# A split-precision transformer layer on one core: three of four right-hand sums of the way down on VectorE, in place, with other slots for the tiles around them

## The chip, the core and the metric

The kernel runs on one core of a Trainium2 chip. The metric is the device time in microseconds (us) of one execution, as the median of several. The engines are TensorE (PE, matrix products), VectorE (DVE), ScalarE (ACT), GpSimd (POOL), and SyncE (SP), which here issues all transfers. Each works through a queue of its own strictly in order and waits for the others by semaphores. Operands lie in an on-chip buffer of 128 partitions; the results of matrix products lie in eight accumulation banks of 128x512 numbers.

## The reference

The program is one layer of a transformer on 1024 tokens of width 1024: two kinds of attention, a gated merge, a normalization, and a feed-forward network (FFN) with a hidden width of 2816. Only the FFN's second half, the "way down", is touched:

```python
g, u = jnp.split(x @ w_ffn_in[l], 2, axis=-1)
ffn = (jax.nn.silu(g) * u) @ w_ffn_out[l]
x = layer_norm(DEEPNORM_ALPHA * x + ffn, ln2_g[l], ln2_b[l])
```

Everything is float32.

## The kernel before

**Split precision.** A float32 product is emulated by three fast ones. Each operand is split into a high part (a cast on ScalarE, line 108) and a low part (the operand minus its high part, on VectorE, line 109), and high x high, high x low and low x high are summed in a bank. The weights of the plain products are split the same way in a helper (line 402 is its subtraction).

**The way up.** The hidden activations h come in 22 tiles f of 128 units (0 to 21). Each is made by seven half-size products instead of eight (the Strassen-Winograd scheme), at line 170 into the banks named sxf, syf and szf. VectorE adds them up at line 183 into the tiles gt and h; lines 830, 833 and 834 are the last steps of silu(g) * u. The left sums of h for the way down are made and written out to a DRAM buffer s_dr in the course of this stage.

**The way down** (lines 906 to 1027) comes in three stages. First plain: f = 0 and 1, eight tiles of tokens x two halves x 6 matmuls, into banks of the tags mm and tr; VectorE evacuates each bank with alpha * x + bank (line 1009). Then four groups of sevens, for f = 2 to 5, 6 to 9, 10 to 13 and 14 to 17. Each group has two pairs of f (named by their first: 2 and 4, 6 and 8, 10 and 12, 14 and 16) and two halves of the tokens; each half runs seven products in the order 1, 2, 6, 5, 7, 3, 4 of 12 matmuls (line 995, banks dx, dy, dz), and VectorE adds each bank to x (line 925). Then plain again: f = 18 to 21, with a normalization for each tile of tokens.

**The right sums.** A seven needs, for each pair of f, the raw weights L (the lower columns of rows f and f+1 of w_ffn_out, side by side) and R (the upper columns), and four sums of them, each split into a high and a low part. The generator right_sums makes them. Before the change it loads L and R into tiles of the tag gt, and POOL makes the four sums (lines 950, 951, 953, 954) in two further tiles, tda and tdb, of the tag yt. The split parts are wdl (raw L), wdb and wda (the sums) and wdc (the upper half of R, raw). The generator stops at each yield; it is moved on by two steps after each tile of the first plain stage and by one step after each product of the sevens, one group ahead.

**The order and the slots.** The order on each engine follows the order of the program text, with a scheduler that moves instructions by their dependencies. All tiles of 128x1024 numbers come from pools by tag, each with so many slots (bw 9, pt 4, yt 3, gt 3, kp 4, xt 16, and qs, kh, kl, v with 2 each, together called QKV). A tile that takes a slot waits until the last reader of the slot's previous tile is done. So the tag of a tile decides what it waits for. The tag gt also holds gt21 of the last f, xt and QKV hold operands of the way up (the products 5 and 7 read theirs, x1S57, from QKV).

Of the kernel before, what the change touches and what calls it, by code (L numbers as in the profile page):

```python
# [26 lines left out]
NF = D_FF // P  # L27
# [4 lines left out]
LO, HI = slice(0, HW), slice(HW, 2 * HW)  # L32
# [14 lines left out]
def hybrid_trunk_kernel(ctx: ExitStack, tc, x, xt, w_in, b_gate, rel_bias, w_proj,  # L47
# [6 lines left out]
    nc = tc.nc  # L54
# [7 lines left out]
    def slot(tag, name, dtype=F32):  # L62
        return pool.tile([P, 1024], dtype, tag=tag, name=name, bufs=SLOTS[tag])
# [8 lines left out]
    QKV = ("qs", "kh", "kl", "v")  # L72
# [34 lines left out]
    def split(dst_h, dst_l, src):  # L107
        nc.scalar.copy(dst_h, src)  # L108
        nc.vector.tensor_tensor(dst_l, src, dst_h.bitcast(F32), ALU.subtract)  # L109
# [571 lines left out]
    for si, (hd, g, st, box) in enumerate(vsteps):  # L681
# [12 lines left out]
        last = goal  # L694
# [182 lines left out]
    for half_k in range(2):  # L877
# [6 lines left out]
        for tt in range(8):  # L884
# [8 lines left out]
            if half_k == 1:  # L893
# [9 lines left out]
              first=3, aside=next_piece)  # L903
# [4 lines left out]
    def load_plain(f0, f1, tags):  # L908
        hs = []
        take = lambda name, dtype: cycle(tags, name, dtype)  # L910
        for f in range(f0, f1):
            hs.append(load_w(h_dr[f], f"h{f}", of("gt"), take, nc.vector) +
                      load_w(w_ffn_out[f * P:(f + 1) * P, :], f"fo{f}", of("gt"), take,
                             nc.vector))
        return hs
# [11 lines left out]
    def right_sums(g, Ws, tags):  # L927

        def take(name):
            return cycle(tags, name, F32R)  # L930

        def split_to(W, key, src, nm):
            W[key] = take(f"{nm}h"), take(f"{nm}l")
            split(*W[key], src)

        def load(W, f, key, cs):
            t = W[key] = slot("gt", f"wd{key}{f}")
            for j, dst in enumerate((LO, HI)):
                dma(t[:, dst], w_ffn_out[(f + j) * P:(f + j + 1) * P, cs])

        sub = ALU.subtract
        put = nc.gpsimd.tensor_tensor
        for f, W in zip(SEVEN[g], Ws):
            load(W, f, "L", LO)
            split_to(W, "hl", W["L"], f"wdl{f}")
            yield
            load(W, f, "R", HI)
            L, R = W["L"], W["R"]
            ta, tb = slot("yt", f"tda{f}"), slot("yt", f"tdb{f}")
            put(ta[:, LO], R[:, LO], L[:, LO], sub)  # L950
            put(tb[:, LO], R[:, HI], ta[:, LO], sub)
            yield
            put(tb[:, HI], L[:, HI], tb[:, LO], sub)
            put(ta[:, HI], R[:, HI], R[:, LO], sub)
            yield
            split_to(W, "hb", tb, f"wdb{f}")
            yield
            split_to(W, "ha", ta, f"wda{f}")
            yield
            c = W["c"] = take(f"wdc{f}")  # L960
            split(c[:, LO], c[:, HI], R[:, HI])
            yield

    def load_left(g, hf):
# [6 lines left out]
    def down_seven(g, hf, Ws, ls, between):  # L971

        bx, by = {}, {}
        key = {1: ("hl", LO), 2: ("hl", HI), 5: ("ha", LO), 7: ("ha", HI), 6: ("hb", LO),
               4: ("hb", HI)}
        for p in ORDER:
            for j in range(2):
                tt = 2 * hf + j
                nm = f"{g}_{tt}"
                up, lo = acc_t[tt], acc_t[tt + 4]  # L980
                if p == 1:
                    bx[j] = bank(("mm", "tr")[hf], f"dx{nm}")
                elif p in (2, 5):
                    by[j] = bank("sc" if p == 5 else ("tr", "pv")[j], f"d{'yz'[p == 5]}{nm}")
                acc = by[j] if p in (2, 5, 3) else bx[j]
                first = p in (1, 2, 5)
                for i, W in enumerate(Ws):
                    if p == 3:
                        wh, wl = W["c"][:, LO], W["c"][:, HI]
                    else:  # L990
                        wh, wl = (w[:, key[p][1]] for w in W[key[p][0]])
                    o = i * HW + j * P
                    lh, ll = ls[p][:, o:o + P], ls[p][:, o + 256:o + 256 + P]
                    for n, (a, b) in enumerate(((lh, wh), (lh, wl), (ll, wh))):
                        mm(acc, a, b, start=(first and i == n == 0), stop=(i == n - 1 == 1),  # L995
                           skip_group_check=not first)
                for dst in {1: [up[:, LO]], 2: [up[:, LO]], 6: [up[:, HI]], 5: [lo[:, HI]],
                            7: [lo[:, HI]], 3: [up[:, HI]], 4: [lo[:, LO]]}[p]:
                    add_to(dst, acc)
            between()  # L1000

    LEFT = ("bw",) * 5 + ("kp",) * 2 + ("bw",) * 4 + ("kp",) * 2
    right_tags = [("xt",) * 14, QKV * 2 + ("pt",) * 4 + ("xt",) * 2]
    first = load_plain(0, 2, ("bw",) * 2 + ("kp",) * 2)
    Wd = [[dict(), dict()] for _ in SEVEN]
    make = right_sums(0, Wd[0], right_tags[0])
    for tt in range(8):
# [6 lines left out]
    for g in range(4):  # L1014
        if g < 3:
            make = right_sums(g + 1, Wd[g + 1], right_tags[(g + 1) % 2])
        for hf in range(2):
# [1 line left out]
            if (g, hf) != (3, 1):  # L1019
                left = load_left(g + hf, 1 - hf)  # L1020
            down_seven(g, hf, Wd[g], ls, lambda: next(make, None))
    last = load_plain(18, NF, ("xt",) * 14 + ("bw",) * 2)
    norm2 = [bcast(src, slot("yt", f"ln2{n}")) for src, n in ((ln2_g, "g"), (ln2_b, "b"))]
    for tt in range(8):
        down_plain(last, tt, add_to)
# [36 lines left out]
```

## Time and profile before

| | before |
|---|---|
| median of 3 runs | 1499.21 us (1498.03 to 1502.22) |
| the profiled execution's own time | 1501.38 us |
| its span in the profile | 1499.3 us |
| mean granted TensorE clock | 0.993 |
| TensorE busy | 1440.3 us, 96% |
| VectorE busy | 1043.9 us, 70% |
| ScalarE busy | 679.7 us, 45% |
| POOL busy | 282.4 us, 19% |

The profile is one execution. Its page gives busy times, the span in 40 slices, and the chain of work that ended last. Beside it stand views of the trace: waits (an engine, the line and tile that waited, what it waited for, us in total, times, longest), the timeline of an engine (start, duration, engine, line, operation, output<-inputs, sizes; in brackets the idle time ahead of it and what ended it), and windows (the busy time of each engine in a stretch, with the granted clock). Buffer numbers are left out of names there: wl_fo is wl_fo0 or wl_fo1. Durations of consecutive instructions of one engine overlap a little; their pitch is read from starts.

### The profile page before, as it was taken

How to read it: one execution, taken by the hardware profiler on the slowest of the kernel's cores; microseconds unless marked ns; L12 is line 12 of the kernel's file. 1: busy time of each engine (PE TensorE's matmuls, PEld its weight loads, DVE VectorE, ACT ScalarE, POOL GpSimd, SP SyncE). 2: the span in 40 equal slices, each digit the busy share in tenths (PEclk: the TensorE clock that was granted, in tenths of full speed). 3: DMA queues.
4: the chain of work that ended last, by engine and by line, in shares of the span. 5: the costliest groups of instructions: out<-in, count | busy, mean ns of one | idle time of the engine just before them, and what ended most of it. 6: DMA issues, size and time to landing. Idle time of an engine off the chain costs nothing. (4 is left out here: it accounts for less than half of the span.)

```text
span 1499.3 us, 19075 instructions
## 1 busy us (share of the span) xinstructions
PE 1440.3 (96%) x6728; PEld 1179.6 (79%) x6728; DVE 1043.9 (70%) x1702; ACT 679.7 (45%) x1174; POOL 282.4 (19%) x322
## 2 busy tenths in 40 slices
PE   8999999999999999899999899999999998999997
PEld 6788888887887777777787688888888886778886
DVE  8865556435878887887849966767777755767757
ACT  6444444336877778775303534444444433111201
POOL 0000000004344558650014000000000003341016
PEclk9999999999999999999999999999999999999999
DMA  6555555247754556647502123444444456677602
GB/s 211 163 175 169 168 168 170 98 144 213 206 170 142 159 165 204 187 157 280 183 0 87 62 100 121 152 155 155 155 155 154 155 189 232 245 249 267 234 8 105
DMA packets 81215, 244.05 MB, mean 163 GB/s; under 512 B 10064, under 2 KB 10064, under 8 KB 81120
## 3 DMA queue, kind: packets, MB, share of 16 engines
q1 hardware_dynamic: 81120, 242.84, 48.5%
q8 instruction: 53, 0.87, 0.2%
q14 instruction: 42, 0.34, 0.1%
HBM read 162.03 MB, written 80.77 MB: 162 GB/s over the span
## 5 line engine op out<-in xcount | busy, mean ns | idle before, releaser
L535 POOL TENSOR_TENSOR w_b<-w_b,kp_b 128x511 f32<-128x511 f32 (+3 forms) x96 | 97.5, 1021 | 51.5 <-DVE kp_b L533 40.6
L950 POOL TENSOR_TENSOR tda<-wdR,wdL 128x512 f32<-128x512 f32 x8 | 10.7, 1340 | 491.6 <-DMA wdR<-in_w_ffn_out_dram 477.8
L533 DVE TENSOR_TENSOR_SCAN kp_b<-kp_b,ident_ps 128x384 f32<-128x384 f32 (+6 forms) x88 | 78.3, 890 | 4.1
L479 POOL MEMSET bias<- 64x64 f32 x8 | 1.2, 146 | 334.5 <-ACT bias L478 334.5
L745 POOL TENSOR_TENSOR mv<-mv,neghalf 128x1 f32<-128x1 f32 x16 | 23.9, 1495 | 211.4 <-DVE mv L744 211.4
L525 ACT ACTIVATE kp_b<-sc_b 128x512 f32<-128x512 f32 (+3 forms) x96 | 48.5, 505 | 31.4 <-PE sc_b L462 26.5
L183 DVE TENSOR_TENSOR c<-sxp,c 128x512 f32<-128x512 f32 x16 | 11.1, 692 | 73.9 <-issue 40.7
L925 DVE TENSOR_TENSOR x<-dx,x 128x512 f32<-128x512 f32 x64 | 43.6, 689 | 24.6 <-PE dx L995 24.6
L109 DVE TENSOR_TENSOR pt_b<-tp_b,pt_b 128x512 fp32r<-128x512 f32 (+1 forms) x96 | 51.1, 543 | 10.9 <-ACT pt_b L108 10.4
L170 PE MATMUL szf<-x1S63h,wcf 128*128 128x512 f32 x176 | 57.8, 389 | 0.0
L500 POOL TENSOR_SCALAR w_a<-w_a,st_a 128x640 f32<-128x640 f32 (+2 forms) x64 | 42.6, 671 | 67.2 <-DVE st_a L499 49.6
L556 PE MATMUL tp_b<-ident,w_b 128*128 128x128 f32 x288 | 49.3, 277 | 5.2 <-DVE pt_b L109 2.8
L108 ACT CAST pt_b<-tp_b 128x512 fp32r<-128x512 f32 (+1 forms) x96 | 47.1, 497 | 13.7 <-PE tp_b L556 13.2
L109 DVE TENSOR_TENSOR sl<-h,sl 128x512 fp32r<-128x512 f32 x56 | 38.4, 686 | 20.2 <-ACT sl L108 20.2
L108 ACT CAST sl<-h 128x512 fp32r<-128x512 f32 x56 | 34.8, 621 | 35.6 <-PE syf L170 17.1
L109 DVE TENSOR_TENSOR pt_a<-tp_a,pt_a 128x512 fp32r<-128x512 f32 (+1 forms) x96 | 45.5, 484 | 7.6 <-ACT pt_a L108 7.3
L497 ACT ACTIVATE w_a<-w_a,st_a 128x640 f32<-128x640 f32 (+2 forms) x64 | 44.6, 698 | 12.8 <-DVE st_a L492 11.2
L118 PE MATMUL ops<-wh_o,ml 128*128 128x512 f32 x128 | 50.2, 392 | 0.2 <-DVE ml L109 0.2
L115 PE MATMUL ops<-wh_o,mh 128*128 128x512 f32 x128 | 50.2, 392 | 0.0
L116 PE MATMUL ops<-wl_o,mh 128*128 128x512 f32 x128 | 49.9, 390 | 0.0
L556 PE MATMUL tp_a<-ident,w_a 128*128 128x128 f32 x240 | 44.8, 277 | 5.0 <-POOL w_a L500 2.4
L833 ACT ACTIVATE h<-sxf 128x512 f32<-128x512 f32 x22 | 13.2, 598 | 79.6 <-PE sxf L170 79.6
(1881 smaller groups left out, 4833.4 us busy)
## 6 DMA issues: line engine op xcount, KB each, us to landing
s_dr<-sl SPq DMA_DIRECT2D x112, 256.0 KB, 2.2
sd<-s_dr SPq DMA_DIRECT2D x56, 512.0 KB, 5.2
wLf<-in_w_ffn_in_dram SPq DMA_DIRECT2D x22, 512.0 KB, 4.4
wRf<-in_w_ffn_in_dram SPq DMA_DIRECT2D x22, 512.0 KB, 3.6
wLp<-in_w_in_dram SPq DMA_DIRECT2D x17, 512.0 KB, 5.3
wRp<-in_w_in_dram SPq DMA_DIRECT2D x17, 512.0 KB, 4.0
v_dr<-v SPq DMA_DIRECT2D x16, 512.0 KB, 4.3
qs<-q_dr SPq DMA_DIRECT2D x16, 512.0 KB, 6.2
```

The lines of the kernel that those rows point to most:

```text
L108: nc.scalar.copy(dst_h, src)
L109: nc.vector.tensor_tensor(dst_l, src, dst_h.bitcast(F32), ALU.subtract)
L115: mm(acc, lh, rh, start=(i == 0), stop=False)
L116: mm(acc, lh, rl, start=False, stop=False)
L118: mm(acc, ll, rh, start=False, stop=(i == n))
L170: mm(acc, lw[:, ks], rx, start=(first and kt == i == 0), stop=(kt == 3 and i == 2), skip_group_check=not first)
L497: nc.scalar.activation(s[:, 0:w], s[:, 0:w], AF.Exp, bias=st[:, m:m + 1], scale=-1.0, accum_out=st[:, 2:3])
L525: nc.scalar.activation(kp[:, c0:e], sc[:, 0:n], AF.Sigmoid, scale=-1.0)
L533: nc.vector.tensor_tensor_scan(kp[:, s0:e], kp[:, s0:e], ident_ps()[:, 0:e - s0], kp[:, s0 - 1:s0], ALU.mult, ALU.bypass)
L535: nc.gpsimd.tensor_tensor(be[:, m0:e], be[:, m0:e], kp[:, m0 - 1:e - 1], ALU.mult)
L556: tr(tp[:, (qb - lo_q) * P:(qb - lo_q + 1) * P], wt[qb - q0][:, (kb - qb) * P:(kb - qb + 1) * P], ident)
L925: nc.vector.tensor_tensor(dst, acc, dst, ALU.add)
```

## The change

Three of the four sums go to VectorE, and all four are made in place. L stays in a gt tile (named wdgt), R goes into a yt tile (named wdyt), both loaded together. The steps, with their lines in the changed kernel: L's lower half becomes R_lower - L_lower (VectorE, 949); R's lower half becomes R_upper - R_lower (POOL, 950); R's upper half becomes R_upper minus the new L_lower (VectorE, 955); L's upper half becomes L_upper minus the new R_upper (VectorE, 956). Since the raw values are overwritten, the split of raw L and that of raw R's upper half (wdc) stand ahead of the sums that overwrite them; wda now is the split of L's tile, wdb that of R's. What is computed is the same.

The slots change too. The eight parts of f = 0 and 1 get tags of their own, so that the high part of w_ffn_out's tile 1 has a bw slot (it took a kp slot before). The left operands (LEFT) take bw and kp in another pattern, the two sets of tags for the right parts are exchanged between even and odd groups, and the last plain weights take QKV, pt and bw instead of xt and bw.

```diff
@@ -933,32 +933,31 @@
             W[key] = take(f"{nm}h"), take(f"{nm}l")
             split(*W[key], src)

-        def load(W, f, key, cs):
-            t = W[key] = slot("gt", f"wd{key}{f}")
+        def load(f, tag, cs):
+            t = slot(tag, f"wd{tag}{f}")
             for j, dst in enumerate((LO, HI)):
                 dma(t[:, dst], w_ffn_out[(f + j) * P:(f + j + 1) * P, cs])
+            return t

         sub = ALU.subtract
-        put = nc.gpsimd.tensor_tensor
+        put = nc.vector.tensor_tensor
         for f, W in zip(SEVEN[g], Ws):
-            load(W, f, "L", LO)
-            split_to(W, "hl", W["L"], f"wdl{f}")
+
+            L, R = load(f, "gt", LO), load(f, "yt", HI)
+            split_to(W, "12", L, f"wdl{f}")
             yield
-            load(W, f, "R", HI)
-            L, R = W["L"], W["R"]
-            ta, tb = slot("yt", f"tda{f}"), slot("yt", f"tdb{f}")
-            put(ta[:, LO], R[:, LO], L[:, LO], sub)
-            put(tb[:, LO], R[:, HI], ta[:, LO], sub)
-            yield
-            put(tb[:, HI], L[:, HI], tb[:, LO], sub)
-            put(ta[:, HI], R[:, HI], R[:, LO], sub)
-            yield
-            split_to(W, "hb", tb, f"wdb{f}")
-            yield
-            split_to(W, "ha", ta, f"wda{f}")
+            put(L[:, LO], R[:, LO], L[:, LO], sub)
+            nc.gpsimd.tensor_tensor(R[:, LO], R[:, HI], R[:, LO], sub)
             yield
             c = W["c"] = take(f"wdc{f}")
             split(c[:, LO], c[:, HI], R[:, HI])
+            yield
+            put(R[:, HI], R[:, HI], L[:, LO], sub)
+            put(L[:, HI], L[:, HI], R[:, HI], sub)
+            yield
+            split_to(W, "54", L, f"wda{f}")
+            yield
+            split_to(W, "76", R, f"wdb{f}")
             yield

     def load_left(g, hf):
@@ -971,8 +970,8 @@
     def down_seven(g, hf, Ws, ls, between):

         bx, by = {}, {}
-        key = {1: ("hl", LO), 2: ("hl", HI), 5: ("ha", LO), 7: ("ha", HI), 6: ("hb", LO),
-               4: ("hb", HI)}
+        key = {1: ("12", LO), 2: ("12", HI), 5: ("54", LO), 4: ("54", HI), 7: ("76", LO),
+               6: ("76", HI)}
         for p in ORDER:
             for j in range(2):
                 tt = 2 * hf + j
@@ -999,9 +998,9 @@
                     add_to(dst, acc)
             between()

-    LEFT = ("bw",) * 5 + ("kp",) * 2 + ("bw",) * 4 + ("kp",) * 2
-    right_tags = [("xt",) * 14, QKV * 2 + ("pt",) * 4 + ("xt",) * 2]
-    first = load_plain(0, 2, ("bw",) * 2 + ("kp",) * 2)
+    LEFT = ("bw",) * 4 + ("kp",) + ("bw",) * 5 + ("kp",) * 3
+    right_tags = [QKV * 2 + ("pt",) * 4 + ("xt",) * 2, ("xt",) * 14]
+    first = load_plain(0, 2, ("bw", "bw", "kp", "kp", "bw", "bw", "bw", "kp"))
     Wd = [[dict(), dict()] for _ in SEVEN]
     make = right_sums(0, Wd[0], right_tags[0])
     for tt in range(8):
@@ -1019,7 +1018,7 @@
             if (g, hf) != (3, 1):
                 left = load_left(g + hf, 1 - hf)
             down_seven(g, hf, Wd[g], ls, lambda: next(make, None))
-    last = load_plain(18, NF, ("xt",) * 14 + ("bw",) * 2)
+    last = load_plain(18, NF, QKV * 2 + ("pt",) * 4 + ("bw",) * 4)
     norm2 = [bcast(src, slot("yt", f"ln2{n}")) for src, n in ((ln2_g, "g"), (ln2_b, "b"))]
     for tt in range(8):
         down_plain(last, tt, add_to)
```

VectorE's queue at the seam between the way up and the way down (f = 21; gt21 and h21 are its tiles; wd*2 and wd*4 are parts of the pairs 2 and 4; wl_fo1 is the low part of w_ffn_out's tile 1; x1_0 is the first tile of tokens), before:

```order
L109 TENSOR_TENSOR wdl2l_11237<-wdL2_11233,wdl2h_11236 128x1024
L109 TENSOR_TENSOR wdb2l_11267<-tdb2_11244,wdb2h_11266 128x1024
L183 TENSOR_TENSOR gt21_11097<-sxf21_11084,gt21_11097 128x512
L109 TENSOR_TENSOR wda2l_11288<-tda2_11243,wda2h_11287 128x1024
L109 TENSOR_TENSOR wdc2_11291<-wdR2_11240,wdc2_11291 128x512
L109 TENSOR_TENSOR wdl4l_11315<-wdL4_11311,wdl4h_11314 128x1024
L183 TENSOR_TENSOR h21_11126<-szf21_11128,h21_11126 128x512
L830 TENSOR_TENSOR h21_11126<-h21_11126,gt21_11097 128x512
L834 TENSOR_TENSOR h21_11126<-h21_11126,gt21_11097 128x512
L402 TENSOR_TENSOR wl_fo1_11212<-wr_fo1_11210,wh_fo1_11211 128x1024
L109 TENSOR_TENSOR wdb4l_11345<-tdb4_11322,wdb4h_11344 128x1024
L1009 SCALAR_TENSOR_TENSOR x1_0_11184<-x1_0_11184,fpswh_h0_11193_0_0_11217 128x512
```

and now, from the same wdl2l on:

```order
L109 TENSOR_TENSOR wdl2l_11240<-wdgt2_11233,wdl2h_11239 128x1024
L183 TENSOR_TENSOR gt21_11097<-sxf21_11084,gt21_11097 128x512
L949 TENSOR_TENSOR wdgt2_11233<-wdyt2_11236,wdgt2_11233 128x512
L109 TENSOR_TENSOR wdc2_11262<-wdyt2_11236,wdc2_11262 128x512
L955 TENSOR_TENSOR wdyt2_11236<-wdyt2_11236,wdgt2_11233 128x512
L183 TENSOR_TENSOR h21_11126<-szf21_11128,h21_11126 128x512
L956 TENSOR_TENSOR wdgt2_11233<-wdgt2_11233,wdyt2_11236 128x512
L830 TENSOR_TENSOR h21_11126<-h21_11126,gt21_11097 128x512
L109 TENSOR_TENSOR wdb2l_11289<-wdyt2_11236,wdb2h_11288 128x1024
L109 TENSOR_TENSOR wda2l_11285<-wdgt2_11233,wda2h_11284 128x1024
L834 TENSOR_TENSOR h21_11126<-h21_11126,gt21_11097 128x512
L1008 SCALAR_TENSOR_TENSOR x1_0_11184<-x1_0_11184,fpswh_h0_11193_0_0_11217 128x512
```

The addition from the bank sxf21 stood behind the split wdb2l; now it stands behind wdl2l alone, with the sums of lines 949, 955 and 956 behind it. wl_fo1 stood behind h21's last step, and is now ahead of these rows.

VectorE's queue in group 1 at the pair 12, before:

```order
L109 TENSOR_TENSOR wdb12l_11932<-tdb12_11896,wdb12h_11931 128x1024
L925 TENSOR_TENSOR x1_1_11185<-dy1_1_11755,x1_1_11185 128x512
L109 TENSOR_TENSOR wda12l_11952<-tda12_11895,wda12h_11951 128x1024
L925 TENSOR_TENSOR x1_0_11184<-dx1_0_11724,x1_0_11184 128x512
L925 TENSOR_TENSOR x1_1_11185<-dx1_1_11732,x1_1_11185 128x512
L109 TENSOR_TENSOR wdc12_11969<-wdR12_11892,wdc12_11969 128x512
```

and now:

```order
L109 TENSOR_TENSOR wdc12_11903<-wdyt12_11848,wdc12_11903 128x512
L925 TENSOR_TENSOR x1_1_11185<-dy1_1_11750,x1_1_11185 128x512
L955 TENSOR_TENSOR wdyt12_11848<-wdyt12_11848,wdgt12_11845 128x512
L925 TENSOR_TENSOR x1_0_11184<-dx1_0_11716,x1_0_11184 128x512
L956 TENSOR_TENSOR wdgt12_11845<-wdgt12_11845,wdyt12_11848 128x512
L925 TENSOR_TENSOR x1_1_11185<-dx1_1_11724,x1_1_11185 128x512
L109 TENSOR_TENSOR wdb12l_11957<-wdyt12_11848,wdb12h_11956 128x1024
```

The evacuation of dy1_1 stood between the splits of two sums, that of dx1_0 behind both; now a subtraction of 128x512 stands between each two evacuations, and the first 128x1024 split of a sum comes behind all of them.

SP's queue, loads of the pair 12 (wd..12) among the left operands (sd), before:

```order
L968 DMA sd1_1_2_11712<-s_dr1_1_1_193 128x1024
L939 DMA wdR10_11763<-in_w_ffn_out_dram 128x512 x2
L968 DMA sd1_1_6_11714<-s_dr1_1_2_194 128x1024
L939 DMA wdL12_11855<-in_w_ffn_out_dram 128x512
L968 DMA sd1_1_5_11716<-s_dr1_1_3_195 128x1024
L939 DMA wdL12_11855<-in_w_ffn_out_dram 128x512
L968 DMA sd1_1_7_11718<-s_dr1_1_4_196 128x1024
L939 DMA wdR12_11892<-in_w_ffn_out_dram 128x512 x2
```

and now:

```order
L967 DMA sd1_1_1_11702<-s_dr1_1_0_192 128x1024
L939 DMA wdgt12_11845<-in_w_ffn_out_dram 128x512 x2
L967 DMA sd1_1_2_11704<-s_dr1_1_1_193 128x1024
L939 DMA wdyt12_11848<-in_w_ffn_out_dram 128x512
L967 DMA sd1_1_6_11706<-s_dr1_1_2_194 128x1024
L939 DMA wdyt12_11848<-in_w_ffn_out_dram 128x512
L939 DMA wdgt14_12018<-in_w_ffn_out_dram 128x512
```

The loads of the pair 12 were issued among the left operands of products 2 to 7 of group 1's second half, one at a time; now all of them stand ahead of the left operands of product 5. The loads of the pair 10 moved likewise: the second half of wdL10 stood behind seventeen loads of left operands (sd0_0_3 to sd1_1_1), and now all of wdgt10 and wdyt10 stands ahead of those.

## The prediction

> **What bounds the kernel now.** The table of busy times comes first: TensorE works for 96% of the span and no other engine comes near. So the time is TensorE's own work, plus the moments when it stops or runs slowly. The change touches only the way down, so I asked next which waits of TensorE lie there, from 1250 us on:
>
> ```profile
> PE 1440.3 (96%) x6728; PEld 1179.6 (79%) x6728; DVE 1043.9 (70%) x1702; ACT 679.7 (45%) x1174; POOL 282.4 (19%) x322
> PE dx L995 <- DVE x L925: 4.6, 3, 3.0
> PE sxf L170 <- DVE gt L183: 3.0, 1, 3.0
> PE fpswh_h L115 <- DVE x L1009: 2.3, 1, 2.3
> PE fpswh_h L116 <- DVE wl_fo L402: 1.1, 1, 1.1
> ```
>
> The last four rows are all of it: 11.0 us in six stops, each ended by VectorE. The timeline gives their places (of the three on L925, the row between these two is the rest, 4.6 - 0.98 - 3.04 = 0.6):
>
> ```profile
> 1256.22 0.72 PE L170 MATMUL sxf<-x1A,wbf21h 128*128 128x512 f32 x2 [2.97 <-DVE gt L183]
> 1269.96 0.50 PE L115 MATMUL fpswh_h<-wh_fo,wh_h 128*128 128x512 f32 x1 [2.27 <-DVE x L1009]
> 1294.62 0.50 PE L995 MATMUL dx<-wdb2h,sd 128*128 128x512 f32 x1 [0.98 <-DVE x L925]
> 1342.46 0.80 PE L995 MATMUL dx<-wda6h,sd 128*128 128x512 f32 x1 [3.04 <-DVE x L925]
> ```
>
> The same stretch by windows (length, busy time of TensorE, its weight loads, VectorE, ScalarE and POOL with counts, granted clock, DMA share, GB/s) shows a second loss, a lower clock behind the longer stops:
>
> ```profile
> 1256.20:1260.70 4.50, 4.48 (x13) 3.56 (x14) 4.13 (x5) 1.05 (x1) 0.20 (x1) 0.62 0.35 112
> 1270.00:1274.40 4.40, 4.40 (x12) 3.45 (x13) 3.43 (x5) 0.47 (x1) 0.00 (x0) 0.61 0.73 262
> 1274.40:1288.00 13.60, 13.60 (x61) 11.25 (x60) 12.47 (x14) 4.17 (x5) 9.29 (x7) 1.00 0.23 78
> 1294.60:1300.00 5.40, 5.38 (x24) 4.45 (x25) 5.30 (x8) 0.00 (x0) 0.00 (x0) 1.00 1.02 416
> 1342.50:1347.10 4.60, 4.60 (x13) 3.70 (x14) 3.57 (x6) 0.00 (x0) 4.06 (x3) 0.63 0.42 129
> ```
>
> After stops of 2.27 to 3.04 us the clock is 0.61 to 0.63 for some 4.5 us; after the stop of 0.98 it stays at 1.00. That costs 0.38 x 4.5 + 0.39 x 4.4 + 0.37 x 4.6 = 5.1 us.
>
> A floor checks this. The chain of waits gives an undisturbed pitch, the timeline the start of f=21's last product, the chain again the start of the last plain stage:
>
> ```profile
> 1252.87 0.39 PE L170 MATMUL szf<-x1S63h,wcf 128*128 128x512 f32 x1
> 1355.22 2.72 PE dy L995 x12
> 1447.70 0.23 PE fpswh_h L115
> ```
>
> The pitch is 2.72 / 12 = 0.2267 us. From 1252.87 + 0.23 = 1253.10 to 1447.70 are 194.6 us, for 12 matmuls of the last up product, 96 of the first plain stage and 4 groups x 2 halves x 7 products x 12 = 672 of the sevens: 780 x 0.2267 = 176.8. So 17.8 us are lost: 11.0 standing, 5.1 at low clock, 1.7 in slow restarts around them. No scheduling in this stretch can bring the span below 1499.3 - 17.8 = 1481.5.
>
> **Why VectorE is late.** Its queue is in order. At the seam:
>
> ```profile
> 1248.07 1.30 POOL L950 TENSOR_TENSOR tda<-wdR,wdL 128x512 f32<-128x512 f32 x1 [420.45 <-DMA wdR<-in_w_ffn_out_dram]
> 1251.94 1.29 POOL L953 TENSOR_TENSOR tdb<-wdL,tdb 128x512 f32<-128x512 f32 x1
> 1253.27 1.05 ACT L108 CAST wdb2h<-tdb 128x1024 fp32r<-128x1024 f32 x1 [4.82 <-POOL tdb L953]
> 1254.34 1.23 DVE L109 TENSOR_TENSOR wdb2l<-tdb,wdb2h 128x1024 fp32r<-128x1024 f32 x1 [6.80 <-ACT wdb2h L108]
> 1255.48 0.68 DVE L183 TENSOR_TENSOR gt<-sxf,gt 128x512 f32<-128x512 f32 x1
> 1262.38 2.20 DVE L402 TENSOR_TENSOR wl_fo<-wr_fo,wh_fo 128x1024 fp32r<-128x1024 f32 x1
> 1268.08 1.23 DVE L109 TENSOR_TENSOR wdb4l<-tdb,wdb4h 128x1024 fp32r<-128x1024 f32 x1 [3.51 <-ACT wdb4h L108]
> 1269.22 2.48 DVE L1009 SCALAR_TENSOR_TENSOR x<-x,fpswh_h 128x512 f32<-128x512 f32 x4
> ```
>
> Four POOL sums in a row, then a cast, then a split that VectorE reached 6.80 us early. The evacuation of sxf is behind it, and TensorE needs that bank. The same with wdb4l ahead of four evacuations (3.51 early), and at group 1:
>
> ```profile
> 1336.82 1.05 ACT L108 CAST wdb12h<-tdb 128x1024 fp32r<-128x1024 f32 x1 [7.02 <-POOL tdb L953]
> 1337.90 1.23 DVE L109 TENSOR_TENSOR wdb12l<-tdb,wdb12h 128x1024 fp32r<-128x1024 f32 x1 [2.30 <-ACT wdb12h L108]
> 1339.64 2.16 DVE L109 TENSOR_TENSOR wda12l<-tda,wda12h 128x1024 fp32r<-128x1024 f32 x1
> ```
>
> **The change, part by part.** *The seam.* Now VectorE reaches the sxf addition behind only wdl2l and the loads of fo0 and fo1, not behind a sum's split. wdl2h needs wdL and a slot that the x1S57 operands free:
>
> ```profile
> 1248.11 0.39 PE L170 MATMUL sxf<-x1S57h,waf21l 128*128 128x512 f32 x1
> 1245.22 1.05 ACT L108 CAST wdl2h<-wdL 128x1024 fp32r<-128x1024 f32 x1 [1.41 <-DMA wdL<-in_w_ffn_out_dram]
> 1256.08 1.22 DVE L109 TENSOR_TENSOR wda2l<-tda,wda2h 128x1024 fp32r<-128x1024 f32 x1
> 1257.22 0.69 DVE L109 TENSOR_TENSOR wdc<-wdR,wdc 128x512 fp32r<-128x512 f32 x1
> ```
>
> Slot free at 1248.5, cast to 1249.75 with a semaphore's delay, split 1.14 (the two starts above) to 1251.0, addition 0.65 to 1251.65. TensorE wants the bank at 1253.1: 1.4 us to spare, so the 2.97 stop goes, with the clock loss behind it. wl_fo1 moves ahead of the seam, since its high part has a bw slot instead of a kp slot that gt21 holds: the 1.06 stop goes.
>
> *The first plain stage.* What VectorE gains as waiting it pays as work: three sums per f on VectorE at 0.60 to 0.69 (no such sum runs there before; the wdc row above is its like, two SBUF operands, 128x512). For f=2 and 4 that is 6 x 0.65 = 3.9 us, against 6.80 + 3.51 = 10.3 of waiting. Run by hand through its new queue from 1251.65: L949, wdc2l, then L955, which waits for POOL's one remaining sum (1252.4 to 1253.7 at the 1.30 of L950); h21's additions and the splits between; the last step of h21 ends at about 1258.4, and the first plain evacuation at about 1260.0, with the bank wanted at 1261.3. VectorE then runs nearly without idling until the eighth tile's first half leaves its bank at 1277.8; TensorE wants it at 1278.9. So the spare is 1.1 to 1.4 us, and about 0.1 where h21 is due at 1258.5. The contended price bounds it: POOL beside VectorE makes a split 2.2 to 2.3.
>
> ```profile
> 1284.11 2.32 DVE L109 TENSOR_TENSOR wdb6l<-tdb,wdb6h 128x1024 fp32r<-128x1024 f32 x1
> L950 POOL TENSOR_TENSOR tda<-wdR,wdL 128x512 f32<-128x512 f32 x8 | 10.7, 1340 | 491.6 <-DMA wdR<-in_w_ffn_out_dram 477.8 <-DVE h L830 7.3 <-DVE x L925 3.9
> L951 POOL TENSOR_TENSOR tdb<-wdR,tda 128x512 f32<-128x512 f32 x8 | 12.0, 1504 | 3.9 <-DMA wdR<-in_w_ffn_out_dram 1.9 <-DVE wda14l L109 1.6
> L953 POOL TENSOR_TENSOR tdb<-wdL,tdb 128x512 f32<-128x512 f32 x8 | 12.4, 1547 | 0.1
> L954 POOL TENSOR_TENSOR tda<-wdR 128x512 f32<-128x512 f32 x8 | 13.3, 1657 | 0.8 <-DMA wdR<-in_w_ffn_out_dram 0.8
> ```
>
> With POOL's work falling from 10.7 + 12.0 + 12.4 + 13.3 = 48.4 to about 11 us I expect two overlaps in the stage, +0.6 each (half of a split's 1.1): 0.1 us over the spare. The 2.27 stop goes, with its clock loss.
>
> *The sevens.* In f=10 and 12 the loads into yt and gt are queued earlier on SP (wdL10's second half stood behind seventeen loads of left operands). A load takes 3.2 us by the median of wdR:
>
> ```profile
> DMA to landing us min/median/max: 2.4/3.2/6.3
> ```
>
> On SP a load into yt waits for the split of the f three before it, and what stands behind it there are left operands wanted about half a group later (84 x 0.2267 = 19 us); POOL's queue holds nothing but its one sum per f. For f=12 both tiles are issued by about 1308 and wanted at 1320, so what remains is VectorE's row: 3 sums and 3 splits spread between evacuations of 0.60 each, no long wait ahead of one. The 3.04, 0.98 and 0.6 stops go. From group 2 on TensorE did not wait before, and VectorE's 12 more sums there, 12 x 0.65 = 7.8 us over two groups of 38.1 (168 x 0.2267), fill idle time. The slots of the last plain weights are free some 20 us early.
>
> *The sum.* Lost before: 17.8. I keep 1.6 of it for what the hand schedule leaves open (0.7 at h21, 0.1 in the plain stage, 0.8 for two short restarts). Gain 16.2. The profiled execution took 1501.38, 2.1 over its span, and 2.2 over the median of 1499.21; taking the gain from the median gives **1483.0**.
>
> [...]
>
> **The rivals.** *One stop stays at the seam*: h21's last step, with 0.1 us of spare, or wdl2h, which waits for a landing and a slot. The 4.82 of ScalarE's idling at wdb2h speaks for late inputs there, the 1.4 us of spare against. Price: 3.0 standing, 1.7 clock, up to 2 behind it: 1487 to 1492. Chance 0.20.
>
> *The clock loss is no consequence of the stops.* Then only the 11.0 goes: 1488. All three slow stretches begin at a stop; 0.04.
>
> *The wait changes its name.* VectorE waits for POOL's remaining sum or for the transfers into yt, as it waited for casts; the kernel then does not do what it says. Against it, POOL's chain is one sum of 1.3 instead of four of 5.2 together. 1495 to 1503; 0.07.
>
> *Slower: VectorE becomes the bound in the first plain stage.* At 1274 to 1288 it is already at 12.47 of 13.60. If the six splits there cost 2.2 instead of 1.1 and the eight sums 1.3, that is 6 x 1.1 + 8 x 0.65 = 11.8 more, less 1.0 of spare, and TensorE, stopping at every bank turn, runs at 0.62 for 22 us: 8.3 more. 19 lost against 17.8, and 5.9 more for each of f=6 and 8 if these crowd too: 1500 to 1512. It decides from the point where VectorE is more than 1.0 us late at a bank turn. Against it: POOL is mostly idle now. 0.07.
>
> **How the numbers follow.** The forecast, 1481 to 1487, has 0.62. Below 1481.5 nothing in the change reaches, beyond the 0.3% between runs; so the low end is 1480.5. The first rival lies inside 1494 with the second, a sum of 0.86 and a little less for the edges. A change is told from none from about 0.3%, 4.5 us: faster 0.86, same 0.07, slower 0.07.
>
> **What would show it.** POOL has 8 sums at L950 and VectorE 24 more; wdb2l no longer follows a wait of 6.80; TensorE shows no wait over 1 us after 1250 and a clock of 1.00 there; the last plain stage starts near 1430 to 1432. I am wrong if a wait of TensorE over 2 us on L183, L925 or the plain evacuation (L1008 now) returns, or if VectorE's splits stand at 2.2 beside idle POOL.

## The result, and the profile after

The changed kernel takes 1483.76 us (median of 4 runs, 1483.2 to 1485.2), the kernel before 1499.26: a ratio of 0.9894 with a 95% interval of 0.988 to 0.9907. The forecast was 1483.0. The profiled execution took 1484.19 us over a span of 1482.3, 17.0 us less than the span before. The medians lie 15.5 us apart.

The page of the profile after, and the windows that answer to the ones shown of before (length, busy time of TensorE, its weight loads, VectorE, ScalarE and POOL with counts, granted clock, DMA share, GB/s):

```profile
PE 1435.9 (97%) x6728; PEld 1178.0 (79%) x6728; DVE 1054.0 (71%) x1726; ACT 679.4 (46%) x1174; POOL 245.2 (17%) x298
1256.20:1260.70 4.50, 4.50 (x22) 3.72 (x21) 4.50 (x6) 2.85 (x4) 0.00 (x0) 1.00 0.89 335
1270.00:1274.40 4.40, 4.40 (x21) 3.66 (x20) 4.40 (x7) 0.00 (x0) 0.00 (x0) 1.00 0.68 228
1274.40:1288.00 13.60, 13.56 (x61) 10.85 (x60) 13.60 (x19) 3.47 (x4) 2.59 (x2) 1.00 0.72 281
1294.60:1300.00 5.40, 5.40 (x25) 4.48 (x24) 3.46 (x6) 0.00 (x0) 0.00 (x0) 1.00 0.74 244
1342.50:1347.10 4.60, 4.60 (x22) 3.82 (x21) 4.60 (x7) 0.00 (x0) 1.29 (x1) 1.00 0.59 202
```

In the three windows that stood at a clock of 0.61 to 0.63 TensorE now starts 21 or 22 matmuls in place of 12 or 13, at 1.00. The view of TensorE's waits has no row at all from 1240 us to the end, where four rows with 11.0 us stood.

One ruler serves for this and all runs below: the time from the start of the last matmul of szf on the way up to the first matmul of the last plain stage. It leaves out the stages ahead, which moved its start between 1250.35 and 1253.80 us. These are its two rows, of the kernel before and then of the changed one:

```profile
1252.87 0.39 PE L170 MATMUL szf<-x1S63h,wcf 128*128 128x512 f32 x1
1447.54 0.39 PE L115 MATMUL fpswh_h<-wh_fo,wh_h 128*128 128x512 f32 x1
```

```profile
1253.17 0.39 PE L170 MATMUL szf<-x1S63h,wcf 128*128 128x512 f32 x1
1430.57 0.39 PE L115 MATMUL fpswh_h<-wh_fo,wh_h 128*128 128x512 f32 x1
```

In between lie 781 matmuls, at the prediction's pitch of 0.2267 us 177.05 us. Before, the stretch took 194.67, so 17.6 us were lost; now it takes 177.40, and 0.35 are lost.

VectorE's queue at the seam and in the first plain stage, after:

```profile
1249.92 1.23 DVE L109 TENSOR_TENSOR wdl2l<-wdgt,wdl2h 128x1024 fp32r<-128x1024 f32 x1 [5.35 <-ACT wdl2h L108]
1251.06 0.68 DVE L183 TENSOR_TENSOR gt<-sxf,gt 128x512 f32<-128x512 f32 x1
1251.66 0.68 DVE L949 TENSOR_TENSOR wdgt<-wdyt,wdgt 128x512 f32<-128x512 f32 x1
1254.13 0.69 DVE L955 TENSOR_TENSOR wdyt<-wdyt,wdgt 128x512 f32<-128x512 f32 x1 [1.18 <-POOL wdyt L950]
1259.41 0.68 DVE L1008 SCALAR_TENSOR_TENSOR x<-x,fpswh_h 128x512 f32<-128x512 f32 x1
1278.70 1.27 DVE L1008 SCALAR_TENSOR_TENSOR x<-x,fpswh_h 128x512 f32<-128x512 f32 x2
```

The addition from sxf no longer has a sum's split ahead of it, and the wait left here is 1.18 us for POOL's one sum, where VectorE waited 6.80 and 3.51 us for casts behind four of them. (One more wait for POOL, of 0.59 us, stands at the pair 12.) From 1254 us on VectorE is full:

```profile
1254.00:1296.00 42.00, 41.86 (x56) 1.00 0.85 314
```

(length, VectorE's busy time, clock, DMA share, GB/s.) It is full, and TensorE beside it does not stop, but for one place, which the timeline of TensorE shows and the view of waits does not list:

```profile
1279.01 0.39 PE L994 MATMUL dx<-wdl4h,sd 128*128 128x512 f32 x1
1279.43 0.50 PE L994 MATMUL dx<-wdl2h,sd 128*128 128x512 f32 x1
```

Here the start comes 0.42 us after the one ahead, not 0.23, and the next two are slower too (0.35 and 0.24 us): product 1's second tile takes the bank of the eighth tile's first half, whose evacuation starts at 1278.70 and ends between 1279.3 (by its pitch) and 1279.4 (by its duration), when the bank is wanted at 1279.24.

### The profile page after: what moved, and what is told of

It reads as the page before. It is cut to its first block, busy times and chain, and to the rows that moved or that the text cites. A ratio compares the mean times of both kernels' runs of the same rounds, so it can differ in the third digit from the quotient of the medians.

```text
span 1482.3 us, 19070 instructions
## 1 busy us (share of the span) xinstructions
PE 1435.9 (97%) x6728; PEld 1178.0 (79%) x6728; DVE 1054.0 (71%) x1726; ACT 679.4 (46%) x1174; POOL 245.2 (17%) x298
## 4 chain that ended last, share of the span: by engine, by line
PE 77%; DVE 11%; ACT 4%; DMA 3%; issue 3%; POOL 2%; SPq 0%; POOLq 0%; DVEq 0%; ACTq 0%
PE sxf L170 15%; PE sxp L170 11%; PE szf L170 8%; PE dx L994 6%; PE szp L170 6%; PE syf L170 4%; PE dz L994 3%; PE syp L170 3%; PE gps L418 2%; DVE kp_b L533 2%; PE ops L118 2%; PE ops L116 2%; PE ops L115 2%; PE fpswh_h L118 1%; PE fpswh_h L115 1%
## 5 line engine op out<-in xcount | busy, mean ns | idle before, releaser
L950 POOL TENSOR_TENSOR wdyt<-wdyt 128x512 f32<-128x512 f32 x8 | 10.9, 1363 | 520.2 <-DVE wdgt L949 501.0
L497 ACT ACTIVATE w_a<-w_a,st_a 128x640 f32<-128x640 f32 (+2 forms) x64 | 44.5, 697 | 12.8 <-DVE st_a L492 11.2
L556 PEld LDWEIGHTS tp_b<-ident,w_b 128*128 128x128 f32 x288 | 34.5, 140 | 18.2 <-DVE pt_b L109 8.3
```

The lines of the kernel that those rows point to most:

```text
L497: nc.scalar.activation(s[:, 0:w], s[:, 0:w], AF.Exp, bias=st[:, m:m + 1], scale=-1.0, accum_out=st[:, 2:3])
L556: tr(tp[:, (qb - lo_q) * P:(qb - lo_q + 1) * P], wt[qb - q0][:, (kb - qb) * P:(kb - qb + 1) * P], ident)
```

## The experiments

The change has three parts that can be told apart: who makes three of the sums (POOL or VectorE); whether the sums are in place, with both loads early and wdc split ahead of them, or apart as before; and the slots. All eight corners were run, two of them being the kernels before and after.

**The new slots alone** (the rest as before):

```diff
-    LEFT = ("bw",) * 5 + ("kp",) * 2 + ("bw",) * 4 + ("kp",) * 2
-    right_tags = [("xt",) * 14, QKV * 2 + ("pt",) * 4 + ("xt",) * 2]
-    first = load_plain(0, 2, ("bw",) * 2 + ("kp",) * 2)
+    LEFT = ("bw",) * 4 + ("kp",) + ("bw",) * 5 + ("kp",) * 3
+    right_tags = [QKV * 2 + ("pt",) * 4 + ("xt",) * 2, ("xt",) * 14]
+    first = load_plain(0, 2, ("bw", "bw", "kp", "kp", "bw", "bw", "bw", "kp"))
...
-    last = load_plain(18, NF, ("xt",) * 14 + ("bw",) * 2)
+    last = load_plain(18, NF, QKV * 2 + ("pt",) * 4 + ("bw",) * 4)
```

> The kernel before with the new slots alone (tags of the first and last plain weights, left operands, right parts); the four sums stay on POOL in tiles of their own. My theory (VectorE's queue stands behind the chain of POOL sums and casts, and moving the sums shortens it): the 2.97 us stop at the seam and the 1.06 us stop at wl_fo1 go, since the addition from sxf and wl_fo1 stand ahead of wdb2l in the new order; but wdb4l still stands ahead of the first plain evacuation, and group 1 keeps its stops of 4.6 us with 1.7 us of low clock: 1492 to 1496 us. Rival (the slots do it, the engine of the sums is indifferent): no wait of TensorE over 1 us from 1250 us on, 1483 to 1486 us.

Measured: 1499.15 us, ratio 0.9992 (0.998 to 1.0005), no difference. The rival fell, but my number was too good by 3 us as well. TensorE's waits and ScalarE's queue; the last row is of the kernel before:

```profile
PE fpswh_h L115 <- ACT h L833: 6.0, 1, 6.0
PE dx L995 <- DVE x L925: 3.3, 2, 2.3
PE dx L995 <- DVE x L1009: 3.0, 2, 1.7
1262.27 1.04 ACT L108 CAST wdb4h<-tdb 128x1024 fp32r<-128x1024 f32 x1 [6.72 <-POOL tdb L953]
1263.22 0.59 ACT L833 ACTIVATE h<-sxf 128x512 f32<-128x512 f32 x1
```

```profile
1260.87 0.60 ACT L833 ACTIVATE h<-sxf 128x512 f32<-128x512 f32 x1 [3.31 <-PE sxf L170]
```

The stops at sxf and wl_fo1 did go, as expected. But POOL's chain now stood in ScalarE's queue: the cast wdb4h waits 6.72 us for POOL, and behind it L833, the last reader of a bank that TensorE wants. In the kernel before L833 ran at 1260.87, ahead of wdb4h at 1267.00. So the new slots changed the order on ScalarE as well, and this stop is of their making. I had looked at VectorE's queue only. The ruler gives 1444.47 - 1252.07 = 192.40, a loss of 15.35.

**The sums moved, the old slots kept** (the diff above, the other way round, on the changed kernel):

> The changed kernel with all slots as before; the sums stay on VectorE, in place. My theory: group 1 runs without stops, as the sums there no longer wait on four POOL sums; at the seam wl_fo1 waits for gt21's slot again, and the first evacuation stands behind wl_fo1, wdc4 and L955: one stop of about 1 us and one of 2 to 3 us with 1.7 us of low clock: 1486 to 1490 us. Rival (the slots do it): 1495 to 1500 us. Second rival (either part alone is enough): 1483 to 1486 us here and with the new slots alone.

Measured: 1485.01 us, ratio 0.9901 (0.9885 to 0.9917). On the ruler 1431.28 - 1250.76 = 180.52, a loss of 3.5.

```profile
PE fpswh_h L116 <- DVE wl_fo L402: 1.4, 1, 1.4
PE fpswh_h L115 <- DVE x L1008: 0.7, 1, 0.7
PE sxf L170 <- DVE gt L183: 0.4, 1, 0.4
```

The time is 1 us below the range expected. These are the waits that were named, with the evacuation's shorter (0.7 for 2 to 3), and without a fall of the clock. Group 1 has no wait.

**The sums back on POOL, everything else as changed**:

```diff
-        put = nc.vector.tensor_tensor
+        put = nc.gpsimd.tensor_tensor
```

> The changed kernel with its four in-place sums all on POOL again. My theory: the chain of four POOL sums of 1.3 to 1.6 us (5.2 to 6 us) plus a cast of 1.05 us is back ahead of wdb2l, wdb4l and the splits of group 1, so VectorE waits in its queue ahead of evacuations: stops of 1 to 3 us return at h21 or the first plain tiles and in group 1, 1487 to 1494 us. Rival (order and slots do it): 1483 to 1486 us.

Measured: 1491.41 us, ratio 0.9942 (0.9924 to 0.996). The ruler: 1437.42 - 1251.15 = 186.27, a loss of 9.2. TensorE's waits, and VectorE's queue ahead of the two longest:

```profile
PE dx L994 <- DVE x L1008: 3.4, 2, 2.8
PE fpswh_h L115 <- DVE x L1008: 1.7, 1, 1.7
PE dx L994 <- DVE x L925: 1.4, 2, 0.8
PE fpswh_h L115 <- ACT h L833: 0.5, 1, 0.5
1265.70 1.34 DVE L109 TENSOR_TENSOR wdb4l<-wdyt,wdb4h 128x1024 fp32r<-128x1024 f32 x1 [2.43 <-ACT wdb4h L108]
1278.03 1.23 DVE L109 TENSOR_TENSOR wda6l<-wdgt,wda6h 128x1024 fp32r<-128x1024 f32 x1 [3.81 <-ACT wda6h L108]
```

VectorE stands again at splits, with evacuations behind. One word decides 8.9 us of the ruler here.

**All four sums on VectorE**:

```diff
-            nc.gpsimd.tensor_tensor(R[:, LO], R[:, HI], R[:, LO], sub)
+            put(R[:, LO], R[:, HI], R[:, LO], sub)
```

> The changed kernel with the fourth sum on VectorE as well, POOL empty on the way down. In the changed kernel VectorE works without a gap from 1254 to 1296 us, and its tightest evacuation there ends 0.6 us ahead of the bank's next use (tile 3's first half ends at 1269.1, wanted at 1269.7). Each pair of f adds 0.6 us of VectorE, but the 1.18 us wait for POOL at the seam goes and the 1.46 us splits beside POOL become 1.2. My theory (spare is enough): no wait of TensorE over 1 us, clock 1.00, 1483 to 1485 us, the same within 0.3%. Rival (VectorE is at its bound there, more work on it stops TensorE at each bank turn): 1488 to 1493 us.

Measured: 1481.91 us, ratio 0.9876 (0.986 to 0.9891), a little below the range expected; no wait of TensorE. The ruler: 1429.21 - 1252.18 = 177.03, nothing lost. More work on a VectorE that was full stopped nothing, since it lost waits at the same time. (The tightest place of the changed kernel was not the one named, 0.6 us ahead, but the eighth tile of the section above, about 0.1 us late.) The row of the split wdc by form shows one of them, in the changed kernel first, in this one second:

```profile
L109 DVE TENSOR_TENSOR wdc<-wdyt,wdc 128x512 fp32r<-128x512 f32 x8 | 9.3, 1161 | 0.4 <-ACT wdc L108 0.4
```

```profile
L109 DVE TENSOR_TENSOR wdc<-wdyt,wdc 128x512 fp32r<-128x512 f32 x8 | 5.5, 686 | 0.4 <-ACT wdc L108 0.4
```

Beside POOL's sum the same split takes 1161 ns, without it 686. So the fourth sum costs VectorE 0.60 us and gives 0.48 back.

**Three sums on VectorE, the rest as before** (tiles of their own, late loads, old slots):

```diff
-        put = nc.gpsimd.tensor_tensor
+        put = nc.vector.tensor_tensor
...
-            put(ta[:, HI], R[:, HI], R[:, LO], sub)
+            nc.gpsimd.tensor_tensor(ta[:, HI], R[:, HI], R[:, LO], sub)
```

> The kernel before, with three of the four sums of each pair on VectorE (lines 950, 951, 953) and nothing else changed: sums in tiles of their own, loads, order of the splits and slots as before. My theory (it is the length of the chain ahead of the casts, four POOL sums of 5 to 6 us in a row, that makes VectorE late): the stop at the seam falls from 3.0 to under 0.5 us, the three stops of group 1 mostly go, wl_fo1 and one evacuation behind it keep about 1 and 2 us: 1486 to 1491 us. Rival (the sums must be in place, with both loads early, before VectorE helps): VectorE now itself waits for the late load of R ahead of evacuations, 1494 to 1500 us.

Measured: 1488.6 us, ratio 0.9916 (0.9901 to 0.9931). The ruler: 1434.21 - 1251.17 = 183.04, a loss of 6.0.

```profile
PE fpswh_h L116 <- DVE wl_fo L402: 3.0, 1, 3.0
PE sxf L170 <- DVE gt L183: 0.8, 1, 0.8
```

Group 1 runs without a wait, with the loads as late as before. What is left is wl_fo1: its stop is now 3.0 us where it was 1.06, though the split itself ends earlier: 10.8 us after the ruler's start (1261.93 - 1251.17) for 11.7 before (1264.58 - 1252.87). The stop of sxf ahead of it, which with its half clock had covered it, is down to 0.8.

**Four sums in place on POOL, old slots** (the diff of the third run and the old slots on the changed kernel):

> The changed kernel with its four in-place sums on POOL and with all slots as before: only the in-place form, the early loads and the new order of the splits are left of the change. The same with the new slots took 1491.4 us (9.2 us lost between the last up product and the last plain stage). My theory: the old slots cost about the 3 us more that they cost with the sums on VectorE: 1492 to 1497 us. Rival (these parts help only together with the new slots): 1498 to 1501 us.

Measured: 1497.37 us, ratio 0.9975 (0.9964 to 0.9987); the ruler 1442.79 - 1252.12 = 190.67, a loss of 13.6. It came out just above my range. The stop at wl_fo1 grows to 4.4 us, in part because the split ends later here, 13.2 us after the ruler's start (1265.29 - 1252.12).

**The changed kernel and all four on VectorE, side by side:**

> The changed kernel once more, to stand beside the next run on the same chip: 1481 to 1485 us, no wait of TensorE from 1250 us on.

> All four sums on VectorE once more, on the same chip as the changed kernel. Both run TensorE without a stop between the last up product and the last plain stage, so my theory is that they are the same and that the 1.9 us between their medians so far come from the stages ahead: within 1 us of the changed kernel. Rival (POOL's sum costs something that the waits don't show): 1.5 to 2.5 us faster than the changed kernel.

Measured on the same chip: 1482.51 us, ratio 0.9871 (0.9856 to 0.9885), and 1482.48 us, ratio 0.9872 (0.9857 to 0.9887). They can't be told apart; the 0.3 us that the ruler gives to the fourth sum (177.35 and 177.03) is below what a time shows here.

**Three sums apart on VectorE, with the new slots:**

> The eighth corner of three choices (sums on POOL or VectorE, apart or in place, old or new slots): three of four sums on VectorE, but in tiles of their own with the loads and the order of the splits as before, and the new slots. Between the last up product and the last plain stage the losses so far are 17.6 us (the kernel before), 15.4 with the new slots, 13.6 in place, 9.2 with both; with the sums on VectorE 6.0 alone, 3.5 in place, 0.4 with both. My theory (VectorE's queue is all, and 3 of the 6.0 us left apart with the old slots are the wait for wl_fo1, which the new slots end): at most 2 us lost, 1482 to 1485 us. Rival (the in-place form is needed, since R apart lands late in a gt slot and VectorE waits for it ahead of an evacuation): 3 us or more lost, 1486 to 1490 us.

Measured: 1481.61 us, ratio 0.9876 (0.9846 to 0.9906), a little below the range expected; no wait of TensorE; the ruler 1427.75 - 1250.35 = 177.40, a loss of 0.35. So the in-place form isn't needed beside the other two parts. The eight corners, in us lost on the ruler:

| sums | apart, old slots | in place, old slots | apart, new slots | in place, new slots |
|---|---|---|---|---|
| on POOL | 17.6 (before) | 13.6 | 15.4 | 9.2 |
| three on VectorE | 6.0 | 3.5 | 0.35 | 0.35 (after) |
| on POOL, without half clock | 12.5 | 11.2 | 13.6 | 9.2 |
| three on VectorE, without half clock | 4.3 | 3.5 | 0.35 | 0.35 |

Each corner is one profiled execution, and part of some losses is time at half clock (half of TensorE's busy time in the slow windows: 5.1, 2.4 and 1.8 us of the first three on POOL, 1.7 of the first on VectorE). The last section shows that how much of it follows a stop depends on where the stop falls in a grid that the program does not set, so the lower two rows leave it out.

Down each column VectorE is worth 8.9 to 15.0 us, and 7.7 to 13.3 without half clock: this is the one part that counts in every setting. The slots are worth 3.1 to 5.6 on VectorE (3.1 to 3.9 without half clock) and 4.4 (2.0) in place on POOL. With the sums apart on POOL their 2.3 is all clock: without it 1.1 us more are lost than before, and the time shows no difference (0.9992). The parts don't add: alone they are worth 11.6 (VectorE), 4.0 (in place) and 2.3 (slots), 17.9 together, where the change gave 17.3, yet VectorE and slots without the third already give all of it.

**A stop of chosen length.** ScalarE copies a bank 11, 13 or 16 times in group 3, where it is idle, and TensorE's order is held; the diff is that for 11 copies, the other two have 13 and 16:

```diff
-                        mm(acc, a, b, start=(first and i == n == 0), stop=(i == n - 1 == 1),
-                           skip_group_check=not first)
+                        ins = mm(acc, a, b, start=(first and i == n == 0),
+                                 stop=(i == n - 1 == 1), skip_group_check=not first)
+                if (g, hf, p, j) == (3, 1, 1, 0):
+                    copies = slot("yt", "copies")
+                    for _ in range(11):
+                        nc.scalar.copy(copies[:, LO], acc)
+                if (g, hf, p, j) == (3, 1, 6, 0):
+                    ctx.enter_context(tc.issue_after(ins.ins))
```

> The changed kernel with a stop of TensorE put into group 3, where ScalarE and POOL are idle: ScalarE copies the bank of product 1's first tile 11 times ahead of product 6, which then has to wait for that bank; TensorE's order is held. At 0.48 us per copy and 4.08 us of matmuls in between the stop is about 11 x 0.48 + 0.2 - 4.1 = 1.4 us. Window theory (the clock falls to 0.50 for one window after a window of a fixed 3.41 us grid in which TensorE stood for about 2 us or more; the profiles so far: 1.72 us in one window didn't do it, 2.19 did): no fall, the time of the changed kernel plus 1.4 us. Length theory (every stop over some 2 us costs 1.7 us of low clock): no fall either. Theory of no connection (the slow stretches of the kernel before had another cause): no fall.

> The same with 13 copies: a stop of about 13 x 0.48 + 0.2 - 4.1 = 2.4 us. Window theory: the clock falls where some 2 us of the stop lie in one window of the grid that the slow stretch near 850 us of the same profile gives, and not where the stop is parted into less; the time is the changed kernel's plus 2.4, in some executions plus 4.1 us. Length theory: a fall always, plus 4.1 us. No connection: no fall, plus 2.4 us.

> The same with 16 copies: a stop of about 16 x 0.48 + 0.2 - 4.1 = 3.8 us. Window theory: a window with over 2 us of standing in most executions (a stop of 3.8 us misses it only if it is parted nearly in the middle), so a fall to 0.50 for 3.4 us at the next edge of the grid; plus 5.5 us in most. Length theory: the same in all. No connection: no fall, plus 3.8 us.

Measured: stops of 3.55, 4.79 and 6.63 us, all longer than meant, since a copy took 0.62 us and not 0.48 (13 took 8.00, in the first row below) and VectorE's addition from the bank came behind the copies; times 1486.42, 1490.96 and 1491.64, ratios 0.9907 (0.9892 to 0.9922), 0.9932 (0.9915 to 0.9949) and 0.9942 (0.9928 to 0.9957). The forecast of no fall with 11 copies missed for that reason. ScalarE's copies in the run with 13; then, in the run with 11, the stop, the window that it mostly fills, and the two after it (length, TensorE's busy time, clock, DMA share, GB/s):

```profile
1413.75 8.00 ACT L999 COPY copies<-dx 128x512 f32<-128x512 f32 x13 [5.80 <-PE dx L994]
```

```profile
1418.53 0.50 PE L994 MATMUL dx<-wdb14h,sd 128*128 128x512 f32 x1 [3.55 <-DVE x L925]
1415.60:1419.00 3.40, 0.47 (x2) 1.00 0.00 0
1419.00:1422.40 3.40, 3.40 (x10) 0.50 0.00 0
1422.40:1425.80 3.40, 3.40 (x16) 1.00 0.00 0
```

The clock fell in all three, for 3.4, 6.8 and 6.8 us. So a stop alone, in a place with no other trouble, makes the slow stretch: the theory of no connection is out. The ruler with 11 copies is 1433.89 - 1251.05 = 182.84, a loss of 5.8; 0.35 is the changed kernel's, 3.55 the stop, 1.7 the half clock over 3.4 us: 5.6. The other two lose 8.3 and 9.4 (1439.13 - 1253.80 and 1437.21 - 1250.75); they lie close together because in the longer stop TensorE stood for 2.1 us of its first slow window too, where a slow clock costs nothing. With all three stops over 3.4 us, these runs do not part the window from the length; the runs below do.

## Why the prediction was right, step by step

**The floor and the losses** held: 17.3 of the 17.6 us came back on the ruler, against a forecast of 16.2 of 17.8. The 1.6 us that I had kept back was sized wrong: 0.35 was lost. The span fell by 17.0, not 17.3, since the changed kernel came to the ruler's start 0.3 us later (1253.17 for 1252.87). The stages ahead move by more than that from one execution to the next, so the floor of 1481.5 holds for this stretch and not for a span: later runs have spans down to 1478.4.

The 1.7 us of slow restarts was what the other terms left over; no row showed it. The run with 11 copies leaves about 0.2 us for one stop. My estimate from that, six stops at 0.2 and the 0.35 that is lost without any, is 1.55.

That the time came out so near 1483.0 is in part luck. The profiled execution of the kernel before took 1501.38, 2.1 us over the median, and I took a gain read from it off the median, which fell by 15.5 only. The 17.0 us by which the spans differ would have given 1482.3 by the same step; what was kept back moved the forecast to 1483.0, nearer to the 1483.76 measured.

**The seam.** The addition from sxf was forecast to end at 1251.65, and ended at 1251.06 + 0.68 = 1251.74; the bank was wanted at 1253.4. The stop of 2.97 is gone. The forecast has 0.2 us of a semaphore's delay between the freed slot and the cast of wdl2h, which no run shows: the last product that reads the slot ended at 1248.41 + 0.39 = 1248.80, and the cast started at 1248.83. The new slots alone end it too, and the sums on VectorE without them leave 0.4 and 0.8 us of it, so either part does most of this work.

The last step of h21 (L834) was to end at 1258.4, with 0.1 us to spare. It ended at 1258.81 + 0.69 = 1259.50, and no stop followed, since it reads no bank. The bank in question is read last by L833, on ScalarE, behind three casts:

```profile
1257.95 0.59 ACT L833 ACTIVATE h<-sxf 128x512 f32<-128x512 f32 x1
```

It is free at 1258.54, and the matmul that takes it (the one that waited for L833 with the new slots alone) starts at 1258.84. So the narrow place was there, with 0.3 us to spare, but in another queue than the one I had worked through.

**wl_fo1.** Right, and more important than I had it. The runs above show that a stop behind a larger one is priced too low by the profile: 1.06 us in the kernel before became 3.0 once the stop ahead was shortened, with the split ending earlier than before. (The slot that wl_fo1's high part waited for is one of the tag kp. That gt21 lies in the tag gt, as the section on the slots has it, is wrong: line 823 takes a kp slot for it.)

**The first plain stage.** L950 was to run from 1252.4 to 1253.7, and ran from 1252.57 for 1.53; the first evacuation was to end at 1260.0, and ended at 1260.09; VectorE was to run nearly without a gap, and did. At the eighth tile's first half the forecast was 0.1 us over the spare, and about 0.2 us were lost. The price of a sum was 0.60 to 0.69, measured 0.68 by 0.60 of pitch. The overlap with POOL was +0.6 in the forecast and about +0.77 measured, on wdc (1.46 for 0.69), not on a 128x1024 split.

**The sevens.** No wait of TensorE, as forecast. The run with the sums apart and late loads shows that the earlier loads of f = 10 and 12, which I counted on, were not needed for it.

**The clock.** The sum was right: three stretches at half clock are gone. The reading was not. I took it that a stop of 2.27 us or more lowers the clock. The run with POOL's sums has a stop of 2.77 us with no such stretch:

```profile
1276.90:1280.30 3.40, 1.98 (x9) 1.00 0.00 1
1280.30:1283.70 3.40, 1.66 (x6) 1.00 0.84 263
1283.70:1287.10 3.40, 3.12 (x14) 1.00 0.94 330
```

The last section tells what decides. For the 5.1 us it made no difference in the profiled execution of the kernel before, where three windows each held 2.27 us of standing or more. In other executions of it that differs: on record it took from 1495.2 us at a mean clock of 0.997 to 1506.19 at 0.990, where the profiled one had 0.993. So the 5.1 us is the loss of that execution, and no fixed price of the stops.

**The rivals.** No long stop stayed at the seam, no wait of TensorE took another name. VectorE did become full, 41.86 of 42.00 us, as the rival on the slow side had it, but the point from which that rival decides, 1.0 us late at a bank turn, was not reached: the worst was 0.2. What I had not seen is ScalarE as a second queue with the same illness (L833 behind wdb4h); it does not show in the kernel before, since L833 stands ahead of wdb4h there.

## What to carry to other kernels

Read an idle engine's wait by what stands behind it in its queue: here a full VectorE (41.86 us busy of the 42.00 from 1254 us on) beats one that waits (33.17 of the 42.00 before), because evacuations stand behind the waits. Price a chain by its whole length, across engines, and look at every in-order queue that it passes through: the new slots alone took two stops away on VectorE and brought a longer one on ScalarE. When parts of a change overlap in what they mend, run the corners: one part alone looked like nothing (0.9992) and was still worth 3 to 6 us beside the other.

## What the runs showed of the clock

The slow stretches of these runs lie on a grid. Read in windows of 0.1 us, every one that ends before its program does lasts 3.4, 6.8 or 10.2 us (to 0.1), and within one execution the distances between their edges are multiples of one period: in the kernel before one ends at 854.3 and others begin at 1257.1, 1270.8 and 1342.4, and (1270.8 - 1257.1) / 4 = 3.43, (1342.4 - 1270.8) / 21 = 3.410 and (1342.4 - 854.3) / 143 = 3.413 us. Its place is not the program's: in two executions of the changed kernel (the second is the one side by side) TensorE starts again at 844.9 and at 844.7, and the slow stretch behind begins at 845.4 and at 847.3. In the slow stretches the clock is 0.50; the 0.61 to 0.63 of the prediction came from windows cut across an edge. Cut along the grid, the kernel before shows the window with the stop, and then the slow one (columns as above):

```profile
1267.40:1270.80 3.40, 1.13 (x6) 1.00 1.02 381
1270.80:1274.20 3.40, 3.40 (x10) 0.50 0.71 260
```

What tells the slow windows here is the standing time within the window ahead. 2.27 us of it lowered the clock (above), and so did 2.19 in the kernel with three sums apart on VectorE, and a single stop of 1.95 ahead of the slow stretch near 850 us, in the changed kernel (second fence):

```profile
1259.80:1263.20 3.40, 1.21 (x5) 1.00 0.82 298
1263.20:1266.60 3.40, 3.40 (x9) 0.51 0.96 343
```

```profile
842.00:845.40 3.40, 1.45 (x6) 1.00 0.00 0
845.40:848.80 3.40, 1.24 (x3) 0.50 0.00 0
```

1.72 us within one window did not (new slots alone):

```profile
1284.40:1287.80 3.40, 1.68 (x8) 1.00 0.00 0
1287.80:1291.20 3.40, 2.13 (x10) 1.00 0.41 112
```

Nor did the stop of 2.77 us, which the edge at 1280.3 parted into 1.40 and 1.37; its second window, with what else stood in it, came to 1.74 (1.75 with the edges read to 0.01 us). So a stop of 1.95 us lowered the clock and one of 2.77 did not, and the length of a stop alone is not what decides. In the traces of the kernel before and of the changed one, from the first record of the clock at 11 and 13 us on, every window at full clock with 1.95 us of standing or more was followed by a slow one, and none with 1.46 or less was. Of the windows read in the other runs 1.92 us is the least that a slow one followed (three sums apart on VectorE, ahead of its slow stretch at 843.4), and 1.75 us (above) is the most behind which none came. So in these runs the limit lies between 1.75 and 1.92 us in 3.41. A stretch lasted longer where the slow window had standing of its own: 0.62 us in it kept the clock low for another window in the run with 13 copies (first fence), 0.06 in the kernel before did not (second). That the window ahead was idle from end to end in the run with 13 copies is not the reason: with the sums in place on POOL and the old slots, TensorE stood for 2.25 us of the window ahead and for 2.15 of the slow one, and a second slow one followed.

```profile
1421.90:1425.30 3.40, 2.78 (x7) 0.50 0.00 0
1425.30:1428.70 3.40, 3.40 (x10) 0.50 0.00 0
```

```profile
1342.40:1345.80 3.40, 3.34 (x8) 0.51 0.22 80
```

For a time this means, as an estimate from that limit, that a single stop of some 1.9 to 3.8 us (once and twice 1.92) costs 1.7 us more (half of 3.41) or not, by where it falls.
